# One TensorE loop over all steps, and output stores held back, in a short-sequence attention kernel

## The chip, the core and the metric

One core of a Trainium2 chip runs the kernel. The metric is the time of one execution in microseconds (us), as the device counts it; lower is better. Each figure comes from several executions, beside executions of the kernel before on the same chip. The profile is one execution; its span, from first to last instruction, is 2.0 to 2.7 us shorter than the time of the same execution. Executions differ by about 1% here (153.42 to 155.17 us for the kernel before). One that is over 1.5% above the fastest of its kernel is called slow and set aside in ratios. The records call the profiled execution of the kernel before slow by this rule, yet its 153.69 us lies within its timed range of 153.42 to 155.17.

## The reference

```python
batch, n_heads, seq, head_dim = 32, 12, 128, 64        # float32 q, k, v
scores = scale * np.matmul(q, k.transpose(0, 1, 3, 2))
attn = np.exp(scores - max(scores)); attn /= attn.sum(-1)
return np.matmul(attn, v)                              # float32
```

There are 384 independent heads: 37.75 MB to read, 12.58 MB to write.

## The kernel before

The work is cut into 48 units of 8 heads and 12 groups of 4 units. GpSimd (POOL) issues the loads of q, k and v, which land as bf16; SyncE (SP) issues the stores. In each step TensorE does four things for different units: transposes of q or k (T), an ordering of v by a selection matrix (V), scores (S) and products (O). ScalarE (ACT) does the exponentials and copies v out of PSUM, the memory that TensorE writes its results to. VectorE (DVE) pairs q or k for the transpose, copies transposes out, and divides by the sum.

TensorE's program has three parts: unrolled first steps, a loop of 5 trips of 8 steps, and an unrolled special end of 8 steps, in which two of the last four v are ordered in the transposes' bank, VectorE copies all four out, and the products of the last two units go to the score banks. Its instructions name fixed buffers, so each buffer count must fit a trip of 8 steps.

```python
vgroups = [4] * (NU // 4 - 1) + [2, 2]          # two small v groups at the end, in slots of their own
PERIOD, LOOP0, TRIPS = 8, 0, 5
...
v_at.setdefault({0: -2, 1: -1, 2: -1}.get(m, m - 3), []).append(m)
NQ, NVB, NVE, NP, NT, NA, NO = 8, 2, 8, 4, 2, 8, 6        # NVB: v buffers, NO: output buffers
...
# SP: a store waits only for the division of its units
op("SP", ("store", c), emit, [("N", first + w) for w in range(n)])
# POOL: loads in one order; a v load waits until TensorE has used the group two earlier
loads.append((t_step[s, j, 0] - 2, "qk"[j], s))
loads.append((vstep_of[m] - 1.5 if m in vstep_of else NU + m, "v", g))
...
def tensor_program():                            # cut
    for i in range(a): run("PE", ops[i], plan[i])
    with nc.tensor.Fori(0, TRIPS):
        for i in range(a, a + size): run("PE", ops[i], plan[i])
    for i in range(b, len(ops)): run("PE", ops[i], plan[i])
```

The softmax here doesn't subtract the row's maximum and nothing guards it: scores larger than these inputs give would overflow.

## Time and profile before

| | before |
|---|---|
| time, median (range) | 154.28 us (153.42 to 155.17) |
| span of the profile | 151.1 us |
| v of units 40 to 43 is there (VectorE's wait for it ends) | 120.3 us |
| TensorE starts step 40 | 127.8 us |
| last multiply on VectorE ends | 146.6 us |
| instruction blocks on queue q8 | 8 |

Two more cuts of this profile matter later. The first is TensorE's timeline in the unrolled end: start, duration, engine, line, operation, output<-inputs, count, and in brackets the idle time before and what ended it (PEq is TensorE's own instruction queue; "issue" means that it waited for nothing that the profile shows). The second is VectorE's last wait for v, and its last instruction.

```profile
127.76 0.61 PE L172 MATMUL qk_ps<-ident,pair 128*128 128x128 bf16 x8
...
132.67 0.61 PE L172 MATMUL qk_ps<-ident,pair 128*128 128x128 bf16 x8 [0.82 <-PEq L551]
...
134.15 1.01 PE L172 MATMUL qk_ps<-ident,pair 128*128 128x128 bf16 x8 [0.51 <-PEq L551]
```

```profile
120.28 0.43 DVE L250 COPY pair<-k_b 128x1024 bf16<-128x1024 bf16 x1 [1.32 <-DMA v_b<-in_v_dram]
...
145.93 0.69 DVE L271 TENSOR_TENSOR o_sb<-s_ps,recip 128x512 f32<-128x512 f32 x1
```

The last three transposes are 4.9 and 1.5 us apart, where the loop takes one each 1.8 us. From step 40 (127.76) to the last multiply's end (146.62) are 18.9 us. I use these two marks for every run: **step 40** says roughly how far the loads let the kernel get, the rest is the **end**. The second mark is a convention: the last load that sets the pace before step 40 is v of units 40 to 43, which arrived 7.5 us earlier.

### The profile page before, as it was taken

What the parts mean: (1) busy time and instruction counts of PE and PEld (TensorE: products, weight loads), DVE (VectorE), ACT (ScalarE), POOL (GpSimd) and SP (SyncE); (2) the same over time, 40 slices, a digit from 0 to 9 for tenths busy, and PEclk for the clock granted to TensorE, in tenths of its full rate; (3) what the DMA queues carried; (4) which work ended last, traced back from release to release, by engine and by line L of the source; (5) the groups of instructions that cost most, each with busy time, mean ns of one, the idle gap of its engine ahead of it and who ended that gap; (6) DMA issues with size and microseconds to landing.
All of it is one profiled execution on the core that took longest, in us unless ns stands there. A gap on an engine that the chain in (4) does not pass through costs nothing. (4 is left out here: it accounts for less than half of the span.)

```text
span 151.1 us, 6998 instructions
## 1 busy us (share of the span) xinstructions
PE 103.6 (69%) x3136; PEld 74.0 (49%) x3136; DVE 92.9 (62%) x208; ACT 72.2 (48%) x93; POOL 27.1 (18%) x42
## 2 busy tenths in 40 slices
PE   0057698836829979919949949949469979557810
PEld 0044465624616756606736736637346657347700
DVE  2163335927726969457667677589096599844770
ACT  3000266618433785734744834838605858714600
POOL 6900014005003232050050050050540000000000
PEclk9999999999996999996995987999955999965995
DMA  2999999996999999999999999999999999971344
GB/s 10 204 202 212 207 211 136 196 234 102 237 228 233 208 203 227 243 239 236 246 236 239 244 237 238 244 235 240 242 235 242 241 239 241 331 240 33 113 138 144
DMA packets 25947, 31.62 MB, mean 209 GB/s; under 512 B 1360, under 2 KB 19792, under 8 KB 25936
## 3 DMA queue, kind: packets, MB, share of 16 engines
q0 software_dynamic: 12880, 18.88, 71.0%
q1 hardware_dynamic: 13056, 12.59, 28.6%
q8 instruction: 8, 0.13, 0.3%
q14 instruction: 3, 0.02, 0.0%
HBM read 37.75 MB, written 12.58 MB: 333 GB/s over the span
## 5 line engine op out<-in xcount | busy, mean ns | idle before, releaser
L233 ACT CAST v_e<-v_ps 128x512 bf16<-128x512 f32 x44 | 25.8, 587 | 63.0 <-PE v_ps L186 63.0
L238 ACT ACTIVATE attnT<-s_ps 128x1024 bf16<-128x1024 f32 x48 | 49.3, 1028 | 6.9 <-PE s_ps L212 6.8
L172 PE MATMUL qk_ps<-ident,pair 128*128 128x128 bf16 x384 | 35.3, 246 | 13.3 <-PEq L551 13.0
L224 PE MATMUL o_ps<-v_e,attnT 128*32 128x65 bf16 x1472 | 22.6, 204 | 26.4 <-PEq L551 18.0
L259 DVE COPY qkT<-qk_ps 128x1024 bf16<-128x1024 bf16 x48 | 32.8, 684 | 6.1 <-PE qk_ps L172 6.0
L172 PEld LDWEIGHTS qk_ps<-ident,pair 128*128 128x128 bf16 x384 | 26.5, 110 | 17.7 <-issue 15.7
L186 PE MATMUL v_ps<-v_b,sel 128*32 128x256 bf16 (+1 forms) x768 | 33.6, 306 | 0.8 <-PEq L551 0.8
L271 DVE TENSOR_TENSOR o_sb<-o_ps,recip 128x512 f32<-128x512 f32 x46 | 31.8, 691 | 1.6
L224 PEld LDWEIGHTS o_ps<-v_e,attnT 128*32 128x32 bf16 x1472 | 16.2, 102 | 32.9 <-issue 29.8
L423 POOL DMA_DIRECT2D v_b<-in_v_dram x13 | 9.7, 752 | 82.7 <-PE v_ps L186 82.7
L250 DVE COPY pair<-k_b 128x1024 bf16<-128x1024 bf16 x24 | 10.8, 454 | 19.4 <-DMA v_b<-in_v_dram 19.1
L186 PEld LDWEIGHTS v_ps<-v_b,sel 128*32 128x32 bf16 x768 | 17.5, 106 | 8.2 <-issue 3.4
L212 PE MATMUL s_ps<-qkT 64*128 64x128 bf16 x384 | 20.9, 236 | 0.0
L268 DVE RECIPROCAL recip<-o_ps 128x8 f32<-128x8 f32 x46 | 9.4, 204 | 17.4 <-PE o_ps L224 17.2
L212 PEld LDWEIGHTS s_ps<-qkT 64*128 64x128 bf16 x384 | 12.1, 101 | 11.0 <-issue 10.7
L250 DVE COPY pair<-q_b 128x1024 bf16<-128x1024 bf16 x24 | 10.3, 431 | 4.6 <-DMA q_b<-in_q_dram 4.5
L438 POOL DMA_DIRECT2D q_b<-in_q_dram x12 | 8.7, 725 | 1.0 <-SPq L93 1.0
L438 POOL DMA_DIRECT2D k_b<-in_k_dram x12 | 8.8, 732 | 0.0
L233 DVE CAST v_e<-v_ps 128x512 bf16<-128x512 f32 x2 | 1.4, 694 | 1.1 <-PE v_ps L186 1.0
L233 DVE CAST v_e<-qk_ps 128x512 bf16<-128x512 f32 x2 | 1.4, 693 | 0.6 <-PE qk_ps L186 0.6
L233 ACT ACT_TABLE_LOAD x1 | 1.3, 1283 | 0.9 <-SPq L93 0.9
L186 PE MATMUL qk_ps<-v_b,sel 128*32 128x128 bf16 x64 | 1.7, 266 | 0.0
(14 smaller groups left out, 6.5 us busy)
## 6 DMA issues: line engine op xcount, KB each, us to landing
out_dram<-o_sb SPq DMA_DIRECT2D x48, 256.0 KB, 8.3
q_b<-in_q_dram POOLq DMA_DIRECT2D x12, 512.0 KB, 13.3
k_b<-in_k_dram POOLq DMA_DIRECT2D x12, 512.0 KB, 16.0
v_b<-in_v_dram POOLq DMA_DIRECT2D x11, 512.0 KB, 11.0
v_b<-in_v_dram POOLq DMA_DIRECT2D x2, 256.0 KB, 19.9
```

The lines of the kernel that those rows point to most:

```text
L172: i = nc.tensor.transpose(p[:, :, r4, jj, :], x[:, r].rearrange("p a d -> p (a d)"), ident[:])
L186: x = nc.tensor.matmul(t[r4 * 32:(r4 + 1) * 32, i, :, :], lhsT=pick[:, w * nh + i, jv, :], rhs=v_b[v_slot(g)][:, :n, (4 * jv + r4) * D:(4 ...
L212: i = nc.tensor.matmul(t[:, a, h, :], lhsT=x[p, 1, 4 * w + h, :], rhs=x[p, 0, 4 * w + h, :], start=True, stop=True)
L224: y = nc.tensor.matmul(t[h * SO:(h + 1) * SO, a, r * (D + 1):(r + 1) * (D + 1)], lhsT=x[:, a, h, r * SO:(r + 1) * SO], rhs=v_e[m % NVE][:, ...
L233: return put(v_e[m % NVE][:, :, :D], v_bank(m).rearrange("p (n e) -> p n e", e=D))
L238: return nc.scalar.activation(out=attnT[u % NA][:].rearrange("p a h (r s j) -> p (a h r) s j", r=4, j=J), in_=s_ps[u % 2][:].rearrange("p ...
L250: return nc.vector.tensor_copy(pair[t_index[t] % NP][:], src[:, 8 * b:8 * b + 8])
L259: return nc.vector.tensor_copy(x.rearrange("p h (r j s) -> p (h r) j s", r=4, j=J)[:, :, 2 * b:2 * b + 2, :].rearrange("p x j s -> p x (j ...
L268: nc.vector.reciprocal(r[:], o4[:, :, :, D]).then_inc(s_r, 1)
L271: return nc.vector.tensor_mul(o[:, :, w, :].rearrange("p a (r d) -> p a r d", d=D), o4[:, :, :, :D], r[:].unsqueeze(3).to_broadcast([128, ...
L423: op("POOL", ("load", kind, x), lambda: nc.gpsimd.dma_start(out=v_b[v_slot(x)][:, :n, :], in_=src,).then_inc(s_v[v_slot(x)], 16), deps)
L438: nc.gpsimd.dma_start(out=t, in_=rows[R][:, n:n + 2, :]).then_inc(sm[x % NQ], 16)
```

## The change

It does two things. TensorE runs all steps in one loop of 7 trips, which branches over the parts that a trip lacks, so fewer instructions should have to be fetched (8 instruction blocks on q8 so far) and the special end goes. Stores go out 14 units late, at unit 36 at the latest, so that loads have the DMA to themselves at first. The core of the diff (cut):

```diff
-    vgroups = [4] * (NU // 4 - 1) + [2, 2]
+    vgroups = [4] * (NU // 4)
-    PERIOD, LOOP0, TRIPS = 8, 0, 5
+    PERIOD = 8
+    TRIPS = NU // PERIOD + 1
...
-        if m < NU - 4:
-            v_at.setdefault({0: -2, 1: -1, 2: -1}.get(m, m - 3), []).append(m)
+        v_at[m - 3] = [m]
-    NQ, NVB, NVE, NP, NT, NA, NO = 8, 2, 8, 4, 2, 8, 6
+    NQ, NVB, NVE, NP, NT, NA, NO = 8, 2, 8, 4, 2, 4, 10
+    LATE, LOADED = 14, NU - 12
...
-        op("SP", ("store", c), emit, [("N", first + w) for w in range(n)])
+        last = first + n - 1
+        op("SP", ("store", c), emit, [("N", max(last, min(last + LATE, LOADED)))])
...
-    (special end of 8 steps: 45 lines)
...
+        nc.tensor.reg_mov(trip, 0)
         with nc.tensor.Fori(0, TRIPS):
-            for i in range(a, a + size):
-                run("PE", ops[i], plan[i])
-        for i in range(b, len(ops)):
-            run("PE", ops[i], plan[i])
+            for skipped, always, some in places:
+                run_waits("PE", always)
+                with nc.tensor.If_ne(trip, skipped):
+                    for o, w in some:
+                        run("PE", o, w)
+            nc.tensor.reg_add(trip, trip, 1)
```

More of the change, by code (lines that the diff above doesn't have):

```diff
@@ L62 @@
     of_unit = {u: s for s, (R, f) in enumerate(supers) for u in range(f, f + R // 4)}
-    PERIOD, LOOP0, TRIPS = 8, 0, 5
-    LOOP1 = LOOP0 + PERIOD * TRIPS
-    TAIL = NU - 8
+    PERIOD = 8
+    TRIPS = NU // PERIOD + 1
     t_at, v_at = {}, {}
@@ L78 @@
     for m in range(NU):
-        if m < NU - 4:
-            v_at.setdefault({0: -2, 1: -1, 2: -1}.get(m, m - 3), []).append(m)
-    for u in v_at:
-        v_at[u].sort()
+        v_at[m - 3] = [m]
     steps = range(min(t_at) - 2, NU + 1)
-    NQ, NVB, NVE, NP, NT, NA, NO = 8, 2, 8, 4, 2, 8, 6
+    NQ, NVB, NVE, NP, NT, NA, NO = 8, 2, 8, 4, 2, 4, 10
+    LATE, LOADED = 14, NU - 12
     def sb(name, shape, dtype):
@@ L97 @@
     k_b = [sb(f"k_b{i}", [128, 2, 16 * D], bf16) for i in range(NQ)]
-    v_b = [sb(f"v_b{i}", [128, 4, RV * D], bf16) for i in range(NVB + 2)]
+    v_b = [sb(f"v_b{i}", [128, 4, RV * D], bf16) for i in range(NVB)]
     v_e = [sb(f"v_e{i}", [128, 8, D + 1], bf16) for i in range(NVE)]
@@ L181, in order_v @@
         nh = 8 // n
-        t = v_bank(m).rearrange("p (i n e) -> p i n e", i=nh, e=D)
+        t = v_ps[:].rearrange("p (i n e) -> p i n e", i=nh, e=D)
         for i in range(nh):
@@ L188, in order_v @@
                         lhsT=pick[:, w * nh + i, jv, :],
-                        rhs=v_b[v_slot(g)][:, :n, (4 * jv + r4) * D:(4 * jv + r4 + 1) * D],
+                        rhs=v_b[g % NVB][:, :n, (4 * jv + r4) * D:(4 * jv + r4 + 1) * D],
                         start=jv == 0, stop=jv == 1)
@@ L206, in scores @@
         w = u - supers[s][1]
-        x = qkT[t_slot(s)]
+        x = qkT[s % NT]
         t = s_ps[u % 2][:].rearrange("p a (h x) -> p a h x", h=4)
@@ L218, in values @@
         x = attnT[u % NA]
-        t = o_bank(u)
+        t = o_ps
         for a in range(2):
@@ L228, in values, with keep_v @@
         return y
-    def keep_v(engine, m):
-        put = nc.scalar.copy if engine == "ACT" else nc.vector.tensor_copy
-        return put(v_e[m % NVE][:, :, :D], v_bank(m).rearrange("p (n e) -> p n e", e=D))
+    def keep_v(m):
+        return nc.scalar.copy(v_e[m % NVE][:, :, :D], v_ps[:].rearrange("p (n e) -> p n e", e=D))
     def exps(u):
@@ L246, in pair_up @@
         src = (q_b, k_b)[j][s % NQ][:].rearrange("p a (r d) -> p r a d", d=D)
-        if supers[s][0] == 8:
-            src = (q_b, k_b)[j][s % NQ][:].rearrange("p a e -> p (a e)")[:, :2 * 8 * D].rearrange(
-                "p (a r d) -> p r a d", a=2, d=D)
         return nc.vector.tensor_copy(pair[t_index[t] % NP][:], src[:, 8 * b:8 * b + 8])
@@ L255, in keep_qk @@
         J = R // 4
-        x = qkT[t_slot(s)][:, j, :R, :]
+        x = qkT[s % NT][:, j, :R, :]
         if J == 2:
@@ L265, in normalise @@
         c, w, n, first = splace[u]
-        o4 = o_bank(u)[:, :, :RO * (D + 1)].rearrange("p a (r e) -> p a r e", e=D + 1)
+        o4 = o_ps[:, :, :RO * (D + 1)].rearrange("p a (r e) -> p a r e", e=D + 1)
         r = recip[u % 2]
@@ L274, in normalise @@
             r[:].unsqueeze(3).to_broadcast([128, 2, RO, D]))
-    def v_bank(m):
-        return qk_ps[:].bitcast(f32) if m in (NU - 3, NU - 1) else v_ps[:]
-    def o_bank(u):
-        return s_ps[u % 2] if u >= NU - 2 else o_ps
-    def t_slot(s):
-        return s % NT
-    def v_slot(g):
-        return g % NVB if vgroups[g] == 4 else NVB + g - (len(vgroups) - 2)
     t_order = [t for u in steps for t in t_at.get(u, [])]
@@ L292 @@
     t_step = {t: u for u in steps for t in t_at.get(u, [])}
-    v_order = [m for u in steps for m in v_at.get(u, [])] + list(range(NU - 4, NU))
-    v_before = {m: v_order[i - 1] if i else None for i, m in enumerate(v_order)}
-    v_engine = {m: "ACT" for m in range(NU)}
-    v_engine.update({m: "DVE" for m in range(NU - 4, NU)})
-    v_looped = {vplace[m][0]: u for u in v_at for m in v_at[u] if vplace[m][1] == 0 and LOOP0 <= u < LOOP1}
     vstep_of = {m: u for u in v_at for m in v_at[u]}
@@ L300 @@
     s_k = [tc.alloc_semaphore(f"s_k{i}") for i in range(NQ)]
-    s_v = [tc.alloc_semaphore(f"s_v{i}") for i in range(len(v_b))]
+    s_v = [tc.alloc_semaphore(f"s_v{i}") for i in range(NVB)]
     s_o = [tc.alloc_semaphore(f"s_o{i}") for i in range(NO)]
-    v_landed, landed, v_readers, slot_users = {}, {}, {}, {}
-    for g in range(len(vgroups)):
-        slot_users.setdefault(v_slot(g), []).append(g)
-        v_landed[g] = (s_v[v_slot(g)], 16 * len(slot_users[v_slot(g)]))
+    v_readers = {}
     for u in range(NU):
@@ L315, in pe_transposes, with pe_wait @@
         op("PE", ("T", t), lambda: transposes(t), deps, ["pe_dve"])
+    def pe_wait(kind, key):
+        op("PE", (kind, None), None, [key])
     def pe_order_v(m):
         g, w, n, first = vplace[m]
-        deps, dma = [], []
-        if m == NU - 3:
-            deps.append(("E", t_order[-1]))
-        elif m >= NU - 2:
-            deps.append(("K", m - 2))
-        elif v_before[m] is not None:
-            deps.append(("K", v_before[m]))
-        if w == 0:
-            if g in v_looped:
-                deps.append(("P", t_at[vstep_of[m]][0]))
-            else:
-                dma.append(v_landed[g])
-        op("PE", ("V", m), lambda: order_v(m), deps,
-           ["pe_act" if v_engine[m] == "ACT" else "pe_dve"], dma)
+        deps = [("K", m - 1)] + ([("P", t_at[vstep_of[m]][0])] if w == 0 else [])
+        op("PE", ("V", m), lambda: order_v(m), deps, ["pe_act"])
     def pe_scores(u):
@@ L343, in pe_values, with act_keep @@
         deps += [("K", m) for m in sorted({v_at_head(u, a, h)[0] for a in range(2) for h in range(4)})]
-        if u < NU - 2:
-            deps.append(("N", u - 1))
+        deps.append(("N", u - 1))
         op("PE", ("O", u), lambda: values(u), deps, ["pe_dve"])
-    def keep(m):
-        e = v_engine[m]
+    def act_keep(m):
         deps = [("V", m)]
@@ L352, in keep @@
             deps += [("O", u) for u in v_readers[m - NVE]]
-        op(e, ("K", m), lambda: keep_v(e, m), deps, ["act_pe" if e == "ACT" else "dve_pe"])
+        op("ACT", ("K", m), lambda: keep_v(m), deps, ["act_pe"])
     def act_exps(u):
@@ L362, in dve_pair @@
         dma = [((s_q, s_k)[j][s % NQ], 16 * (s // NQ + 1))]
-        for g, u in v_looped.items():
-            if t_at[u][0] == t:
-                dma.append(v_landed[g])
+        for m in v_at.get(t_step[t], []):
+            g, w, n, first = vplace[m]
+            if w == 0:
+                dma.append((s_v[g % NVB], 16 * (g // NVB + 1)))
         op("DVE", ("P", t), lambda: pair_up(t), deps, ["dve_io"] if t_index[t] else ["dve_pe", "dve_io"], dma)
@@ L371, in dve_keep @@
         for x in range(s):
-            if t_slot(x) == t_slot(s):
+            if x % NT == s % NT:
                 R, f = supers[x]
@@ L381, in dve_normalise @@
             dma.append((s_o[c % NO], sum(16 * pieces(x) for x in range(c % NO, c, NO))))
-        marks = ["dve_pe"] if u < NU - 3 else []
-        if u + 1 > TAIL:
-            marks = marks + ["dve_io"]
+        marks = ["dve_pe"] + (["dve_io"] if u + 8 > t_step[t_order[-1]] else [])
         op("DVE", ("N", u), lambda: normalise(u), [("O", u)], marks, dma)
@@ L412, in pool_load @@
         if kind == "v":
-            users = slot_users[v_slot(x)]
-            i = users.index(x)
-            if i:
-                g = users[i - 1]
-                first = sum(vgroups[:g])
-                deps = [("V", first + w) for w in range(vgroups[g])]
+            if x >= NVB:
+                deps = [("V", sum(vgroups[:x - NVB + 1]) - 1)]
             n, first = vgroups[x], sum(vgroups[:x])
-            src = v_rows[:, first:first + n, :]
-            if n == 2:
-                src = v_rows[:, NU - 4:, :].rearrange("p (a w) e -> p w a e", a=2)[:, (first - NU + 4) // 2]
             op("POOL", ("load", kind, x), lambda: nc.gpsimd.dma_start(
-                out=v_b[v_slot(x)][:, :n, :], in_=src,
-            ).then_inc(s_v[v_slot(x)], 16), deps)
+                out=v_b[x % NVB][:, :n, :], in_=v_rows[:, first:first + n, :],
+            ).then_inc(s_v[x % NVB], 16), deps)
             return
@@ L434, in emit @@
         def emit():
-            t = bufs[x % NQ][:]
-            if R == 8:
-                t = t.rearrange("p a e -> p (a e)")[:, :2 * R * D].rearrange("p (a e) -> p a e", a=2)
-            nc.gpsimd.dma_start(out=t, in_=rows[R][:, n:n + 2, :]).then_inc(sm[x % NQ], 16)
+            nc.gpsimd.dma_start(
+                out=bufs[x % NQ][:], in_=rows[R][:, n:n + 2, :]).then_inc(sm[x % NQ], 16)
         op("POOL", ("load", kind, x), emit, deps)
-    step_starts = {}
+    op("ACT", ("K", -1), lambda: nc.scalar.drain(), [], ["act_pe"])
+    at_step = {}
     for u in steps:
-        step_starts[u] = len(program["PE"])
-        if u >= TAIL:
-            continue
+        start = len(program["PE"])
         for t in t_at.get(u, []):
             pe_transposes(t)
+        if u == t_step[t_order[-1]] + 1:
+            pe_wait("T", ("E", t_order[-1]))
         for m in v_at.get(u, []):
             pe_order_v(m)
-            keep(m)
-        if u == -1:
-            pe_scores(0)
-            act_exps(0)
-        if 0 <= u:
+            act_keep(m)
+        if u - 1 == vstep_of[NU - 1]:
+            pe_wait("V", ("K", NU - 1))
+        if 0 <= u + 1 < NU:
             pe_scores(u + 1)
             act_exps(u + 1)
+        if 0 <= u < NU:
             pe_values(u)
@@ L465 @@
             dve_keep(t)
-        if u + 2 <= TAIL:
-            for t in t_at.get(u + 2, []):
-                dve_pair(t)
-    def tail_scores(u):
-        pe_scores(u)
-        act_exps(u)
-    t45, t46, t47 = t_order[-3:]
-    u = TAIL
-    dve_normalise(u - 1)
-    pe_transposes(t45)
-    dve_keep(t45)
-    pe_order_v(u + 3)
-    tail_scores(u + 1)
-    pe_values(u)
-    dve_normalise(u)
-    keep(u + 3)
-    dve_pair(t46)
-    tail_scores(u + 2)
-    pe_values(u + 1)
-    dve_pair(t47)
-    tail_scores(u + 3)
-    dve_normalise(u + 1)
-    pe_transposes(t46)
-    dve_keep(t46)
-    pe_values(u + 2)
-    pe_transposes(t47)
-    dve_keep(t47)
-    dve_normalise(u + 2)
-    pe_values(u + 3)
-    tail_scores(u + 4)
-    tail_scores(u + 5)
-    dve_normalise(u + 3)
-    pe_order_v(u + 4)
-    keep(u + 4)
-    pe_order_v(u + 5)
-    keep(u + 5)
-    tail_scores(u + 6)
-    pe_values(u + 4)
-    dve_normalise(u + 4)
-    pe_order_v(u + 6)
-    keep(u + 6)
-    tail_scores(u + 7)
-    pe_values(u + 5)
-    pe_order_v(u + 7)
-    keep(u + 7)
-    dve_normalise(u + 5)
-    pe_values(u + 6)
-    dve_normalise(u + 6)
-    pe_values(u + 7)
-    dve_normalise(u + 7)
+        for t in t_at.get(u + 2, []):
+            dve_pair(t)
+        for o in program["PE"][start:]:
+            at_step[o.key] = u
     for c in range(len(stores)):
@@ L528 @@
         m = sum(vgroups[:g])
-        loads.append((vstep_of[m] - 1.5 if m in vstep_of else NU + m, "v", g))
+        loads.append((vstep_of[m] - 1.5, "v", g))
     loads.sort(key=lambda e: e[0])
@@ L546, in waits_of, with run_waits @@
         return out
+    def run_waits(engine, waits):
+        for name, value in waits:
+            i = ENGINE[engine].wait_ge(sems[name], value)
+            if engine == "PE":
+                i.then_inc(sems[name], -value)
     def run(engine, o, waits):
         e = ENGINE[engine]
-        for name, value in waits:
-            i = e.wait_ge(sems[name], value)
-            if engine == "PE":
-                i.then_inc(sems[name], -value)
+        run_waits(engine, waits)
         for s, value in o.dma:
@@ L560, in tensor_program @@
     def tensor_program():
-        ops = program["PE"]
-        a, b = step_starts[LOOP0], step_starts[LOOP1]
-        assert (b - a) % TRIPS == 0
-        size = (b - a) // TRIPS
-        plan = [waits_of("PE", o) for o in ops]
-        for i in range(a, b):
-            assert not ops[i].dma and plan[i] == plan[a + (i - a) % size], (ops[i].key, plan[i])
-            assert ops[i].key[0] == ops[a + (i - a) % size].key[0]
-        for i in range(a):
-            run("PE", ops[i], plan[i])
-        with nc.tensor.Fori(0, TRIPS):
-            for i in range(a, a + size):
-                run("PE", ops[i], plan[i])
-        for i in range(b, len(ops)):
-            run("PE", ops[i], plan[i])
+        ops, waits, when = {}, {}, {}
+        for o in program["PE"]:
+            place = at_step[o.key] % PERIOD, o.key[0]
+            w = waits_of("PE", o)
+            assert waits.setdefault(place, w) == w and not o.dma, (o.key, w, waits[place])
+            when.setdefault(place, []).append((at_step[o.key] // PERIOD + 1, o.emit is None))
+            if at_step[o.key] // PERIOD == 2:
+                ops[place] = o
+        places = []
+        for place in [(l, kind) for l in range(PERIOD) for kind in "TVSO"]:
+            trips = [t for t, empty in when[place] if not empty]
+            assert trips in (list(range(TRIPS - 1)), list(range(1, TRIPS))), (place, trips)
+            waiting = len(when[place]) > len(trips)
+            assert not waiting or len(when[place]) == TRIPS
+            skipped = 0 if trips[0] else TRIPS - 1
+            if waiting or not places or places[-1][0] != skipped:
+                places.append((skipped, waits[place] if waiting else [], []))
+            places[-1][2].append((ops[place], [] if waiting else waits[place]))
+        trip = ctx.enter_context(nc.tensor.register("trip"))
+        nc.tensor.reg_mov(trip, 0)
+        with nc.tensor.Fori(0, TRIPS):
+            for skipped, always, some in places:
[4 more added lines that the diff above has]
+            nc.tensor.reg_add(trip, trip, 1)
     with nc.Block() as block:
```

## The prediction

> **What bounds the kernel now.** I read the 40 slices first, then 5 us windows over the whole span, then the waits, then TensorE's timeline. The page's slices of data movement and the queues:
>
> ```profile
> DMA  2999999996999999999999999999999999971344
> GB/s 10 204 202 212 207 211 136 196 234 102 237 228 233 208 203 227 243 239 236 246 236 239 244 237 238 244 235 240 242 235 242 241 239 241 331 240 33 113 138 144
> q0 software_dynamic: 12880, 18.88, 71.0%
> q1 hardware_dynamic: 13056, 12.59, 28.6%
> q8 instruction: 8, 0.13, 0.3%
> ```
>
> A slice is 3.78 us. The DMA engines are full from slice 1 to slice 34 (about 132 us), with a hole at slice 9, then mostly idle for the last 19 us. q0 is the loads (18.88 MB as they land in bf16), q1 the stores (12.59 MB). The windows (columns: stretch, length, busy us and count of PE, PEld, DVE, ACT, POOL, granted clock, DMA share, GB/s) give the rates:
>
> ```profile
> 5.00:10.00 5.00, 1.78 (x16) 1.55 (x16) 2.12 (x4) 0.00 (x0) 2.66 (x4) 1.00 1.14 204
> 10.00:15.00 5.00, 3.24 (x35) 2.00 (x32) 2.35 (x5) 0.00 (x0) 0.00 (x0) 1.00 1.16 211
> 15.00:20.00 5.00, 3.68 (x50) 2.29 (x51) 1.84 (x4) 1.77 (x4) 0.00 (x0) 1.00 1.18 208
> ...
> 95.00:100.00 5.00, 3.04 (x99) 2.10 (x99) 2.75 (x7) 3.67 (x5) 2.00 (x3) 1.00 1.14 241
> ...
> 130.00:135.00 5.00, 2.58 (x88) 2.11 (x88) 2.96 (x6) 2.74 (x4) 0.00 (x0) 0.86 1.00 338
> 135.00:140.00 5.00, 3.29 (x114) 2.87 (x112) 2.89 (x6) 1.91 (x2) 0.00 (x0) 0.50 0.14 43
> 140.00:145.00 5.00, 3.65 (x220) 2.76 (x212) 4.04 (x9) 2.08 (x3) 0.00 (x0) 0.95 0.23 76
> 145.00:150.00 5.00, 0.00 (x0) 0.00 (x0) 1.55 (x4) 0.00 (x0) 0.00 (x0) 0.73 0.62 210
> ```
>
> The first store is issued at 25.0 us, so the first three rows are loads alone: mean 208 GB/s. 130 to 135 us is stores alone: 338 GB/s. Mixed 1.5 to 1 these rates give 1/(0.6/208 + 0.4/338) = 246 GB/s, and 235 to 246 is what the middle shows: **load time and store time simply add up.** Loads cost 18.88/0.208 = 90.8 us, stores 12.59/0.338 = 37.2 us, 0.78 us for each of the 48 units. The first 5 us moved 54 x 5 = 0.27 MB, as if loading began at 3.7 us. A DMA that never idled would end at 3.7 + 90.8 + 37.2 = 131.7 us. The span is 151.1 us, so 19.4 us are DMA idleness, over half of it after 135 us, where TensorE and VectorE finish the last units and there is nothing to move.
>
> In the middle, compute waits for loads (the waits):
>
> ```profile
> POOL v_b L423 <- PE v_ps L186: 82.7, 9, 14.5
> DVE pair L250 <- DMA v_b<-in_v_dram: 19.1, 9, 3.7
> ```
>
> Each group of 4 units waits once, about 2 us, for its v load; POOL can issue that load only when TensorE has used the group two earlier. TensorE's timeline shows its pace and its instruction stalls:
>
> ```profile
> 29.42 0.34 PE L224 MATMUL o_ps<-v_e,attnT 128*32 128x65 bf16 x19
> 32.84 0.30 PE L224 MATMUL o_ps<-v_e,attnT 128*32 128x65 bf16 x13 [3.08 <-issue]
> ...
> 62.08 0.43 PE L224 MATMUL o_ps<-v_e,attnT 128*32 128x65 bf16 x32
> 62.67 0.61 PE L172 MATMUL qk_ps<-ident,pair 128*128 128x128 bf16 x8 [0.16 <-PEq L551]
> ...
> 125.89 0.61 PE L172 MATMUL qk_ps<-ident,pair 128*128 128x128 bf16 x8
> ```
>
> In the first trip the 32 products of one step stop in the middle, with nothing in the program to wait for: 0.65, 3.08, 1.68 and 3.02 us, in steps 1, 3, 5 and 7, after 23, 19, 15 and 11 products. Later trips never do it. Free of waits a step takes 1.80 us.
>
> [...] A load packet is 1466 bytes (18.88 MB/12880), 7.0 us per 1000 packets at 208 GB/s, a store packet 964 bytes, 2.9 us, so where both queues are full I estimate that loads get some 70% of the time. [...] q8 is 8 packets of 16 KB; the stalls lie two steps apart, and two steps are some 264 instructions; the loop of some 1056 stalls only in its first trip. From entering one block (the end of the former stall) to the arrival of the next I read 6.8, 5.4 and 6.8 us under load. [...] The back edge in the trace: from the start of one step's products to the next step's transposes is normally 0.36 us, but 0.59 us at 62.08 and 0.58 at 85.42 and 105.59, so about 0.2 us is exposed once a trip.
>
> **The change part by part.**
>
> 1. *One loop of 7 trips.* Merging neighbours with the same condition leaves 12 branches a trip (one for steps 0 to 2 of the trip, two each in steps 3 and 4, three in step 5, two each in steps 6 and 7). [...] In the middle this is hidden: 4 steps take 7.2 us of compute against some 10.9 us of DMA. It shows in the first 14 steps, where loads alone allow 90.8/12 = 7.6 us per 4 steps: I charge 2 us. It also shows in the last steps: 1 us. Instruction blocks fall from 8 to 5 or 6, and the 8.4 us of mid-group stalls go: that fetching moves into trip 0, partly under the wait for the first load.
>
> 2. *The start.* v unit 0 now goes through the copy of step -3, which must wait for the v load. Before, its products started at 13.95 us, when that load was in; the transpose of that step began at 11.13. Chaining 1.0 us pieces from there[...] I get scores of unit 0 at 20.3 us instead of 19.3, and the last block of the loop, fetched from about 16 us on, comes at about 22: another 2 us. The fourth v is then ordered at about 25 us instead of 21.8, and with it the ninth load is issued. The first 8 loads last till 3.7 + 8 x 2.52 = 24 us. So the DMA is dry for about 3 us, where before it lost 1 to 2 us here and 2 us more at 35 to 40 us (141 GB/s instead of 241). Call it even, with 4 us idle in the start and point 1 together.
>
> 3. *Stores held back.* A chunk goes out 14 units late, but at unit 36 at the latest. Till unit 36 stores of 22 units are out (17.1 us of DMA); 14 units go out in one burst there, 12 follow. The bytes are the same; they leave the stretch in which loads gate compute and fill the one in which the DMA was idle. The 10 output buffers cover it: a buffer is needed again 5 steps (13 us) after its store was issued, and the median store lands in 8.3 us.
>
> 4. *The end.* The last v load (units 44 to 47) now waits for v of unit 39, because two equal slots replace the two small extra ones, so it competes with the burst. When it lands, loads (90.8 us), 22 units of stores (17.1) and some 3 units of the burst (2.4) have passed: 3.7 + 110.3 + 5 us idle (4 from point 2, 1 in between) = **119 us**. From there VectorE has three full steps at 1.80 us and six at about 1.65 (products 0.5 until the reciprocal, 0.93 for it and the multiply, some 0.2 for the wait back), 15.3 us, plus 1 us of branches. Then the last store: 4.5 us, as from 146.6 to 151.1 now. Sum 119 + 15.3 + 1 + 4.5 = 139.8. The DMA's own end: 23 units left at 0.78 us = 17.9 us, 137. The two ends nearly meet, and the special ending that used both score banks for products (steps of 1 us) isn't missed much. I take a span of **139 us**, 12 less than now. Time minus span was 153.69 - 151.1 = 2.6 us in the profiled run, 3.8 for the median; 3 more gives **142 us**.
>
> **The rivals.**
>
> *Stores were hidden anyway.* If the loads had gaps, holding stores back would free nothing: the end would move only by the restructured tail, 150 to 157 us. Against it: DMA share at 1.1 and more, and rates that add up.
>
> *Instruction fetch becomes the bound in trip 0.* The taken branches may each stall for a block, not only the last; three or four stalls at 5.4 to 6.8 us instead of one short one would delay the start by up to 10 us: 148 to 152 us. [...] Against: the first load lands only at 6.8 us and early DMA traffic is light.
>
> *The end becomes a new wait.* If the burst starves the last v load, or VectorE waits for an output buffer that is still being stored, the last steps slip by 3 to 5 us: 145 to 147. For it: stores of 3.67 MB (10.9 us) stand in the queue at that moment. Against: the estimated 70% share, and the load is half way at least.
>
> *The loads-only phase is compute-bound.* Branches at 0.3 us or more would idle the DMA another 3 us: 145.
>
> **Range and chances.** Everything well (no dry DMA at the start, branches hidden) gives 3.7 + 128 + about 2 for the last receipt = 134 of span, 137 of time. One of the last three rivals gives 145 to 148. So 8 in 10: 136.5 to 148. Faster by over 2% (under 151.8) needs a quarter of the expected gain: 0.93; within 2%: 0.05; slower: 0.02.
>
> **What would show it.** q8 with 5 or 6 packets; no mid-group stop after step 0; 208 GB/s till the first store at about 50 to 55 us, then about 240, then 300 and more from about 112 us almost to the end, DMA slices full till the last two; VectorE's last wait for v at about 119 us; the last unit's multiply at about 135. It is wrong if the DMA is dry for more than 5 us early (fetch, late ninth load), if the last v lands after 124 us, or if a wait for stores shows up on VectorE.

## The result

The changed kernel takes 144.36 us (143.38 to 145.38, 4 runs) against 154.28 us. The ratio is 0.9357, with a 95% interval of 0.9258 to 0.9456: faster. A ratio here is the mean time of one kernel's fast runs over that of the other's of the same rounds, so not quite the ratio of the medians quoted.

The slices (now 3.53 us each) and queues of the changed kernel:

```profile
DMA  2999999699999999999999999999999999999982
GB/s 14 186 206 211 202 206 179 81 210 188 181 200 143 212 189 187 219 176 235 246 236 240 253 236 240 252 235 242 253 235 241 255 206 313 379 382 369 335 281 77
q0 software_dynamic: 12864, 18.88, 76.5%
q1 hardware_dynamic: 13056, 12.59, 28.0%
q8 instruction: 4, 0.07, 0.2%
```

The DMA now works until two slices before the end. The first store is issued at 57.1 us. In the windows the last stretch moves stores alone, faster than I had read before:

```profile
20.00:25.00 5.00, 4.43 (x92) 2.89 (x92) 1.60 (x4) 2.42 (x4) 0.59 (x1) 0.66 0.95 179
25.00:30.00 5.00, 4.80 (x161) 3.37 (x158) 4.90 (x11) 3.89 (x6) 1.56 (x3) 1.00 0.85 130
...
40.00:45.00 5.00, 3.74 (x141) 2.79 (x145) 4.90 (x12) 2.87 (x5) 2.02 (x3) 1.00 0.97 165
...
120.00:125.00 5.00, 3.42 (x108) 2.47 (x112) 3.41 (x8) 2.20 (x4) 0.00 (x0) 1.00 1.09 380
```

But the loads-only stretch has dips (130 and 165 GB/s), though nothing but loads is there to move. The waits (total, times, longest) show why loads are not ordered faster, and one new wait, for output buffers:

```profile
POOL v_b L381 <- PE v_ps L185: 83.4, 10, 16.7
...
DVE pair L245 <- DMA v_b<-in_v_dram: 20.2, 12, 2.9
...
DVE recip L263 <- DMA out_dram<-o_sb: 6.3, 6, 2.1
```

TensorE's timeline has one stop in the middle of a group, in the step before step 0, in place of four; step 40 begins at 120.07 us:

```profile
20.57 1.04 PE L185 MATMUL v_ps<-v_b,sel 128*32 128x256 bf16 x15 [2.15 <-issue]
...
120.07 0.61 PE L171 MATMUL qk_ps<-ident,pair 128*128 128x128 bf16 x8 [0.46 <-PEq L458]
```

VectorE's timeline shows the arrival of v of units 40 to 43, that of the last v load and the last multiply:

```profile
110.36 0.43 DVE L245 COPY pair<-k_b 128x1024 bf16<-128x1024 bf16 x1 [1.67 <-DMA v_b<-in_v_dram]
...
121.25 0.43 DVE L245 COPY pair<-k_b 128x1024 bf16<-128x1024 bf16 x1 [1.33 <-DMA v_b<-in_v_dram]
...
136.17 0.69 DVE L266 TENSOR_TENSOR o_sb<-o_ps,recip 128x512 f32<-128x512 f32 x1
```

So of the 9.8 us of span, 7.7 are gained on the way to step 40 (127.76 to 120.07) and 2.1 in the end (18.9 to 16.8 us). The split depends on the mark: v of units 40 to 43 is there 9.9 us earlier (120.28 and 110.36), and from there to the last multiply's end both kernels take much the same, 26.3 and 26.5 us. By that mark the whole gain lies ahead of it, and the end gains nothing. The last store takes 4.4 us (4.5 before). Which part of the change bought them is what the experiments ask.

### The profile page after: what moved, and what is told of

It is laid out like the page before. It is cut to its first block, busy times and chain, and to the rows that moved or that the text cites. A ratio compares the mean times of both kernels' runs of the same rounds, so it can differ in the third digit from the quotient of the medians.

```text
span 141.3 us, 6998 instructions
## 1 busy us (share of the span) xinstructions
PE 97.5 (69%) x3072; PEld 68.9 (49%) x3072; DVE 89.8 (64%) x204; ACT 74.2 (52%) x97; POOL 26.8 (19%) x41
## 3 DMA queue, kind: packets, MB, share of 16 engines
q0 software_dynamic: 12864, 18.88, 76.5%
## 5 line engine op out<-in xcount | busy, mean ns | idle before, releaser
L231 ACT CAST v_e<-v_ps 128x512 bf16<-128x512 f32 x48 | 28.2, 588 | 58.4 <-PE v_ps L185 58.4
L171 PE MATMUL qk_ps<-ident,pair 128*128 128x128 bf16 x384 | 32.5, 233 | 16.5 <-PEq L458 15.7
L185 PE MATMUL v_ps<-v_b,sel 128*32 128x256 bf16 x768 | 33.0, 295 | 3.1 <-issue 2.1
L171 PEld LDWEIGHTS qk_ps<-ident,pair 128*128 128x128 bf16 x384 | 24.3, 104 | 21.5 <-issue 20.6
L266 DVE TENSOR_TENSOR o_sb<-o_ps,recip 128x512 f32<-128x512 f32 x48 | 33.2, 691 | 1.7
L223 PE MATMUL o_ps<-v_e,attnT 128*32 128x65 bf16 x1536 | 21.7, 200 | 18.2 <-PEq L458 18.1
L381 POOL DMA_DIRECT2D v_b<-in_v_dram x12 | 9.2, 770 | 83.4 <-PE v_ps L185 83.4
L245 DVE COPY pair<-k_b 128x1024 bf16<-128x1024 bf16 x24 | 11.0, 460 | 20.2 <-DMA v_b<-in_v_dram 20.2
L211 PE MATMUL s_ps<-qkT 64*128 64x128 bf16 x384 | 19.9, 226 | 0.6 <-PEq L458 0.5
L211 PEld LDWEIGHTS s_ps<-qkT 64*128 64x128 bf16 x384 | 11.3, 97 | 11.5 <-issue 11.5
```

The source lines that it names most:

```text
L171: i = nc.tensor.transpose(p[:, :, r4, jj, :], x[:, r].rearrange("p a d -> p (a d)"), ident[:])
L185: x = nc.tensor.matmul(t[r4 * 32:(r4 + 1) * 32, i, :, :], lhsT=pick[:, w * nh + i, jv, :], rhs=v_b[g % NVB][:, :n, (4 * jv + r4) * D:(4 * ...
L211: i = nc.tensor.matmul(t[:, a, h, :], lhsT=x[p, 1, 4 * w + h, :], rhs=x[p, 0, 4 * w + h, :], start=True, stop=True)
L223: y = nc.tensor.matmul(t[h * SO:(h + 1) * SO, a, r * (D + 1):(r + 1) * (D + 1)], lhsT=x[:, a, h, r * SO:(r + 1) * SO], rhs=v_e[m % NVE][:, ...
L231: return nc.scalar.copy(v_e[m % NVE][:, :, :D], v_ps[:].rearrange("p (n e) -> p n e", e=D))
L245: return nc.vector.tensor_copy(pair[t_index[t] % NP][:], src[:, 8 * b:8 * b + 8])
```

## The experiments

All gave correct results. They ran in four sets (e1 to e3 and e5; e4, its control, e6 and e7; e8 to e10; e11), on three chips; each set has its own runs of the kernel before, so compare ratios. "Step 40" is the start of its transposes, "end" the time from there to the last multiply's end, both from the one profiled run.

| run | median us | before us | ratio (95%) | step 40 | end |
|---|---|---|---|---|---|
| kernel before | 154.28 | | 1 | 127.8 | 18.9 |
| changed | 144.36 | 154.28 | 0.936 (0.926 to 0.946) | 120.1 | 16.8 |
| e1 loop, not held | 151.08 | 153.19 | 0.981 (0.972 to 0.990) | 128.6 | 16.9 |
| e2 held, no loop | 152.28 | 153.19 | 0.995 (0.984 to 1.006) | 125.4 | 20.2 |
| e3 held 7 | 147.31 | 153.19 | 0.962 (0.954 to 0.969) | 123.3 | 17.8 |
| e5 14 buffers | 143.19 | 153.19 | 0.927 (0.916 to 0.937) | 119.7 * | 17.9 * |
| e6 first steps out | 146.73 | 154.39 | 0.949 (0.932 to 0.966) | 121.9 | 16.9 |
| e10 the same, not held | 151.92 | 154.20 | 0.991 (0.983 to 0.999) | 129.3 * | 18.0 * |
| e7 held 20 | 143.60 | 154.39 | 0.932 (0.922 to 0.943) | 116.0 | 16.4 |
| e8 q, k earlier | 144.03 | 154.20 | 0.941 (0.935 to 0.946) | 120.0 | 15.5 |
| e9 both e6 and e8 | 148.44 | 154.20 | 0.971 (0.963 to 0.979) | 124.4 | 15.5 |

(* profiled run called slow.) Three more runs are told below. The granted clock of TensorE differs between the runs too: 0.90 to 0.95 in the four of the changed kernel, 0.85 to 0.90 in those of e1. Within e1 the run with the higher clock is the faster (149.86 us at 0.900, 152.53 at 0.849), within the changed kernel it is not (143.77 at 0.902, 145.38 at 0.923). What the clock adds to small differences was not separated.

### e1: the loop alone

```diff
-    LATE, LOADED = 14, NU - 12
+    LATE, LOADED = 0, NU - 12
```

> The changed kernel with stores issued at once (no unit of delay), TensorE still in one loop. Theory A (the stores that are held back pay: their DMA time moves from the load-bound stretch into an idle end; the loop is about neutral): the last v load lands 39 units of stores into the run instead of 25, 3.7 + 90.8 + 30.4 + 5 idle = 130 us, then 15.6 us of steps and 4.4 us of last store: span 150, time 150 to 156. Theory B (the single loop pays: no stops for instructions in the first trip, a smoother end): time stays at 144 to 147.

Measured: 151.08 us, span 149.7; the last v load at 129.8 us. Theory A expected just that. Without the holding, the loop (with the v groups and buffer counts that come with it) is worth 1.9%. Where, its one profile doesn't settle: its span is 1.4 us shorter. From step 40 the end is 2.0 us shorter (16.9 against 18.9) and step 40 comes 0.8 later; but v of units 40 to 43 is there 1.3 us earlier (118.98 against 120.28), and from there both take much the same, 26.5 and 26.3 us.

### e2: the holding alone

The kernel before with the `LATE` lines, 10 output buffers, and VectorE's signals to SP placed as in the changed kernel (cut):

```diff
+    LATE, LOADED = 14, NU - 12                     # and NO = 10
-        op("SP", ("store", c), emit, [("N", first + w) for w in range(n)])
+        last = first + n - 1
+        op("SP", ("store", c), emit, [("N", max(last, min(last + LATE, LOADED)))])
```

> The kernel before with only the stores held back 14 units (till unit 36) and 10 output buffers; TensorE keeps its unrolled first and last steps and its four stops for instructions. Theory A: most of the gain is here, 141 to 147 us, the loads end about 118 us. Theory B: 152 to 155.

Measured: 152.28 us, ratio 0.995, not clear of 1. Theory A was wrong here: holding alone gains almost nothing. Yet e1 had refuted theory B. **The parts do not add: 0.5% and 1.9% alone, 6.4% together.** In its profile e2 is 4.7 us ahead of the kernel before when v of units 40 to 43 is there, and gives 3.6 of them back after that: 29.9 us to the last multiply's end, against 26.3.

```profile
115.60 0.43 DVE L252 COPY pair<-k_b 128x1024 bf16<-128x1024 bf16 x1 [1.67 <-DMA v_b<-in_v_dram]
```

The slices of e2 (3.76 us each):

```profile
GB/s 7 203 198 214 205 213 157 195 151 19 182 209 20 146 210 166 188 185 240 236 248 244 237 238 243 237 240 242 237 242 240 237 244 349 382 381 381 170 161 118
```

Slices 9 and 12 move almost nothing, and TensorE's timeline has stops just ahead of them:

```profile
26.10 0.26 PE L226 MATMUL o_ps<-v_e,attnT 128*32 128x65 bf16 x9 [0.92 <-issue]
...
33.20 0.30 PE L226 MATMUL o_ps<-v_e,attnT 128*32 128x65 bf16 x13 [3.33 <-issue]
...
44.58 0.51 PE L226 MATMUL o_ps<-v_e,attnT 128*32 128x65 bf16 x21 [2.62 <-issue]
```

Between 20 and 50 us e2 moves 136 GB/s, the changed kernel 176: over 30 us that is 1.2 MB, or 5.8 us of loading at the 208 GB/s of the first stretch. Both have only loads to move there. The kernel before moves 200 GB/s in the same stretch and e1 202, because stores fill up what loads leave. By queue it is plainer (`--dma --window 20:50`): the kernel before loads 3.96 MB there and e2 4.01, with no store in the way; e1 loads 4.33 and the changed kernel 5.27. So e2 takes the stores out of this stretch and puts holes in their place. That the stops are fetches of instructions the trace shows: in the kernel before, the packets of the instruction queue (q8) start at 23.67, 30.41, 35.87 and 42.67 us, and TensorE goes on 2.3 to 2.4 us after each, at 26.00, 32.84, 38.28 and 45.05. My theory for the next runs (C) was that these stops make the holes.

### e3: half the delay

```diff
-    LATE, LOADED = 14, NU - 12
+    LATE, LOADED = 7, NU - 12
```

> The changed kernel with a delay of 7 units instead of 14. Theory A: linear, 8 more units of stores (30 instead of 22) lie ahead of the last v load, 8 x 0.78 = 6 us: 148.5 to 151, last v at about 127. If the gain has a threshold (loads only need some of the relief), 144 to 146.

Measured: 147.31 us; the last v load at 124.8 us. Not held, held 7 and held 14 have the ratios 0.981, 0.962 and 0.936: 1.9 and 2.6 points for 7 units each, with intervals of 1 point on each. (The medians, 151.08, 147.31 and 144.36, come from two sets and give 3.8 and 2.9 us, the other way round.) Within the one-loop kernel the holding pays about evenly; no threshold shows. The time is 1.2 us under theory A's range, and the last v load came 2.2 us earlier than it said.

### e5: enough output buffers

```diff
-    NQ, NVB, NVE, NP, NT, NA, NO = 8, 2, 8, 4, 2, 4, 10
+    NQ, NVB, NVE, NP, NT, NA, NO = 8, 2, 8, 4, 2, 4, 14
```

> The changed kernel with 14 output buffers instead of 10, so that VectorE no longer waits for stores (6.3 us in 6 waits in the trace). Theory A: these waits lie ahead of a wait for v that would come anyway, so the time stays 143 to 145.5. Rival: they hold TensorE back and with it the next v load: 139 to 142.

Measured: 143.19 us (141.23 to 144.69). The waits for stores are gone from the list, but its interval overlaps that of the changed kernel, and it has runs on both sides of theory and rival. A gain of 1% from more buffers is neither shown nor excluded; a gain anywhere near the 6.3 us of waiting is excluded.

### e6 and e10: the first steps out of the loop

The first steps stand unrolled ahead of a loop of 6 trips with 6 branches each, so that the loop's blocks are fetched in steps 0 to 7 again, as before the change. The end stays in the loop. e10 is e6 with `LATE = 0`.

```diff
-        with nc.tensor.Fori(0, TRIPS):
+        for o, w in prefix:
+            run("PE", o, w)
+        nc.tensor.reg_mov(trip, 1)
+        with nc.tensor.Fori(0, TRIPS - 1):
             for skipped, always, some in places:
                 run_waits("PE", always)
+                if skipped == 0:
+                    for o, w in some:
+                        run("PE", o, w)
+                    continue
```

> The changed kernel, but TensorE's steps before step 0 stand unrolled ahead of the loop (6 trips, 6 branches a trip), as before the change; stores stay held back, the last steps stay in the loop. So the loop's instruction blocks are again fetched during steps 0 to 7. Theory C (held stores leave the DMA nothing to do while TensorE stops for instructions, which is why holding alone gained only 0.5%): three or four stops of 1 to 3.5 us in the middle of a group come back, the transposes of step 40 start about 5 us later than the 120.1 us of the changed kernel, time 147.5 to 150. Rival D (the unrolled end is what spoiled the kernel that only held back; the stops at the start don't matter): 143.5 to 145.5.

> Steps before the loop unrolled (stops for instructions in steps 0 to 7), stores not held back, last steps in the loop. With the three others of this kind it makes a square: stops or none, held or not. Theory C (stops hurt only where no stores fill the DMA): it is within 1 us of the single loop without holding (151.1): 150 to 152. If stops cost the same with and without holding: 153 to 154.5.

Measured: 146.73 us for e6, 151.92 for e10. The stops came back in e6, and the holes with them (slices of 3.6 us; slices 9 and 12 again):

```profile
GB/s 7 194 206 211 207 205 203 207 175 63 209 171 28 206 206 133 198 228 235 236 234 245 235 240 243 238 244 245 235 240 244 237 238 289 381 379 380 381 291 26
```

```profile
24.16 0.27 PE L223 MATMUL o_ps<-v_e,attnT 128*32 128x65 bf16 x10 [1.05 <-issue]
30.69 0.30 PE L223 MATMUL o_ps<-v_e,attnT 128*32 128x65 bf16 x15 [2.60 <-issue]
...
41.49 0.39 PE L223 MATMUL o_ps<-v_e,attnT 128*32 128x65 bf16 x25 [2.05 <-issue]
```

But they delay step 40 by 1.8 us, not by the 5 that theory C needed (by ratio the two kernels' intervals overlap), and e6 keeps most of the gain of holding (146.73 against 151.92). The reason is that the loop pays for its instructions too, only earlier. The ninth load, which waits for TensorE, is ordered at 20.8 us in e6 and at 24.4 in the changed kernel, after the single stop; eight steps later (two v loads on) it is 43.95 against 39.80. So e6 loses 7.8 us in steps 0 to 7 but starts 3.6 us earlier. The four runs make a square:

| | stops in steps 0 to 7 | one stop, before step 0 | difference |
|---|---|---|---|
| not held | 151.92 (e10) | 151.08 (e1) | 0.8 us |
| held 14 | 146.73 (e6) | 144.36 (changed) | 2.4 us |

By ratios the differences are 1.0 and 1.3 points, with intervals of 1 point and more on each, so this square does not show that stops hurt more when stores are held. **Theory C, as the whole cause of e2, falls.** The stops make the holes, but they are the smaller part of what e2 lacks. By queue, holding lets 0.70 MB more of loads through between 20 and 50 us with the stops (e10 4.02, e6 4.72) and 0.94 without (e1 4.33, changed 5.27), where in the unrolled kernel it let through 0.05 more.

What separates e2 from e6 (152.28 and 146.73 us, both held, both with stops)? The profiles give two parts. The end: 20.2 us against 16.9 (the special end with held stores against the plain one; the special end without them took 18.9). And step 40: 125.4 against 121.9. That second difference is there at once: the ninth load is ordered at 22.3 us against 20.8, and two v loads later it is 47.5 against 44.0; from there to the order of v of units 40 to 43 both take 57 us. e2 differs from e6 ahead of that point, as far as I see, in the placement of the first v orderings (steps -2, -1, -1 against -3, -2, -1), in the length of its stops (6.9 us against 5.7 in all) and in the buffers of the exponentials. How much belongs to each was not separated.

### e7: held longer

```diff
-    NQ, NVB, NVE, NP, NT, NA, NO = 8, 2, 8, 4, 2, 4, 10
-    LATE, LOADED = 14, NU - 12
+    NQ, NVB, NVE, NP, NT, NA, NO = 8, 2, 8, 4, 2, 4, 14
+    LATE, LOADED = 20, NU - 12
```

> Stores held back 20 units, with 14 buffers. If load time and store time simply add up, 6 units fewer lie ahead of the last v load: it lands 4 to 5 us earlier (116 to 118). But 32 units of stores then have to drain behind it: 32 x 0.69 us at 380 GB/s are 22 us, so the end is set by stores, 141 to 144 (hardly a gain). If the loads-only stretch is bound by TensorE and VectorE instead of the DMA, the last v load comes less than 2 us earlier and the time is 143 to 145.

Measured: 143.60 us, ratio 0.932, no different from 14 units. In its profile the last v load and the last multiply come 4 to 5 us earlier than in the changed kernel, but the span is 141.6 us, 0.3 more:

```profile
116.93 0.43 DVE L245 COPY pair<-k_b 128x1024 bf16<-128x1024 bf16 x1 [1.12 <-DMA v_b<-in_v_dram]
...
131.67 0.69 DVE L266 TENSOR_TENSOR o_sb<-o_ps,recip 128x512 f32<-128x512 f32 x1
```

From the last multiply to the end are now 9.2 us, which the DMA spends on the heap of stores. The buffers alone (e5, held 14) had shown no clear gain. Fourteen is about where the end of compute and the end of the stores meet; beyond it the gain turns into a wait for stores.

### e4 and its control: three v buffers

The dips of the changed kernel in the loads-only stretch come, I thought, from v loads that wait for one of two buffers. With three, the loop body must be 12 steps long:

```diff
-    PERIOD = 8
+    PERIOD = 12
-    NQ, NVB, NVE, NP, NT, NA, NO = 8, 2, 8, 4, 2, 4, 10
+    NQ, NVB, NVE, NP, NT, NA, NO = 8, 3, 12, 4, 3, 4, 10
```

> The changed kernel with three v buffers (and, so that one loop body fits, trips of 12 steps, three transposed buffers, 12 v outputs). Theory E (the DMA dips to 130 GB/s at 25 to 30 us and 165 at 40 to 45 because a v load is ordered only when the group two earlier has been used): the dips go, the last v lands earlier, 138 to 141.5. Rival: TensorE's larger body (1600 instructions, 7 blocks) costs in trip 0 what that brings: 144 to 147.

> Control of the one above: the same three buffers and 12-step trips, but each v load still waits for the group two earlier. Its distance to the changed kernel is the price of the larger body (0 to +3 us: 144 to 147.5), its distance to the one above is the worth of ordering v one group earlier (theory E: 4 to 6 us; rival: under 1).

Measured: 153.43 us, and 153.74 for the control, whose v loads wait for the group two earlier as in the changed kernel. Both miss every expectation. The queue and TensorE's timeline of e4:

```profile
q8 instruction: 12, 0.20, 0.5%
```

```profile
36.52 0.40 PE L185 MATMUL v_ps<-v_b,sel 128*32 128x256 bf16 x2 [2.90 <-issue]
...
48.41 0.51 PE L185 MATMUL v_ps<-v_b,sel 128*32 128x256 bf16 x11 [1.98 <-issue]
...
61.08 0.82 PE L171 MATMUL qk_ps<-ident,pair 128*128 128x128 bf16 x6 [4.48 <-issue]
```

Twelve blocks instead of 4, and stops on till 61 us. The longer body costs some 9 us (153.74 against 144.36); under that, the third buffer shows nothing. What it would be worth without the longer body stays open.

### e8, e9 and e11: a fuller queue of loads

The same idea without another buffer: q and k loads (8 buffers each) are ordered one group earlier, so that they do not stand behind the v load that waits.

```diff
-            loads.append((t_step[s, j, 0] - 2, "qk"[j], s))
+            loads.append((t_step[s, j, 0] - (2 if s < 3 else 6), "qk"[j], s))
```

> The changed kernel with one line different: from the fourth on, q and k loads are ordered one group (4 steps) earlier, so that they no longer stand behind the v load that waits for a slot; the first loads keep their order. Theory E (the DMA runs dry at 20 to 30 and 40 to 45 us because loads queue up behind that wait): 10 loads instead of 8 carry it to 29 us, the dips to 81 and 143 GB/s go, the transposes of step 40 start at 116 to 118 instead of 120.1 us, time 140 to 142.5. Rival: a v load now lands later because more stands ahead of it, and TensorE waits for it as long as it gained: 143.5 to 146.

> The same line, on the kernel with the steps before the loop unrolled (146.7 us). If the stops for instructions cost time only by drying up the queue of loads, a fuller queue takes most of their cost away: 141 to 143.5, as good as the one above or better, for its start is 3.6 us earlier. If they cost time by delaying TensorE itself, 145 to 147.

Measured: 144.03 us for e8, which is the rival's number. The slices of e8 (3.54 us each) and VectorE's last wait for v:

```profile
GB/s 13 194 198 206 208 206 211 211 207 211 205 212 128 191 208 163 191 176 232 234 243 246 236 237 245 238 238 244 239 237 248 237 151 237 380 380 380 379 307 8
```

```profile
120.10 0.43 DVE L245 COPY pair<-k_b 128x1024 bf16<-128x1024 bf16 x1 [0.29 <-DMA v_b<-in_v_dram]
```

The early dips are gone: 205 GB/s and more from slice 3 through 11, and 198 GB/s from 20 to 50 us against 176, which is 0.66 MB or 3.2 us of loading ahead. But step 40 starts where it did (120.0 us). The lead lay in q and k buffers. v, which decides, stood behind them: the fifth v load is ordered at 43.6 us instead of 39.8. And when q and k had run out, the last v load was alone in the queue and the DMA partly idle (125 GB/s from 112 to 118 us).

e9, with the first steps out of the loop as well, took 148.44 us, no better than e6 with 146.73 (by ratio 0.971 against 0.949, intervals that just overlap). So a fuller queue does not take away the price of the stops. That they delay TensorE itself, and cost more with q and k ahead of v, fits but was not shown. That was neither of the two numbers expected.

The last run let the stores of e8 go at unit 34 to fill the late hole:

```diff
-    LATE, LOADED = 14, NU - 12
+    LATE, LOADED = 14, NU - 14
```

> q and k ordered one group earlier, and the held stores let go at unit 34 instead of 36. In the kernel that only ordered q and k earlier the early dip was gone, but from 112 to 118 us the DMA moved 35 to 223 GB/s: the last v load stood alone there and the burst came 2 to 3 us too late. Theory E (each us of an idle DMA before the last store costs a us): the burst at about 109.6 us fills the hole, DMA and compute end 1.5 to 2 us sooner, 141 to 143 us. Rival: the burst now slows the v load before the last and moves everything behind it: 144 to 146.

Measured: median 144.1 us (141.44 to 146.02, 7 runs) against 155.24 us. The hole was filled only in part (150 GB/s instead of 125 in that stretch) and step 40 starts at 120.3 us. The ratio of its fast runs is 0.912, but only 3 of 7 runs count as fast; the ratio of the medians is 0.928. Whether it beats the changed kernel by 1% or not at all is not settled.

## Why the prediction was right, and where its steps failed

The time (144.4 us for 142 predicted) lies in the range, and the direction and size are right. By its steps (the last 3 us of the sum, from span to time, were a little too many: the 3.8 us for the median took one execution's span from another's time; each execution's own gap is 2.0 to 2.7 us, 2.1 in the profiled run):

- **The end.** Right. From the last v load to the last multiply's end I added 15.3 us and 1 us for branches; it took 15.6 (121.25 to 136.86). The steps there took 1.6 us each (products at 128.74, 130.34, 131.92, 133.49), and the last store 4.4 for 4.5. (The "about 2 for the last receipt" in the prediction's range is in the trace of the kernel before: its last bytes move at 149.05 us and the span ends at 151.12, 2.1 us later.) "The special ending isn't missed much" holds: from step 40 the special end took 18.9 and 20.2 us in its two profiles, the plain one 15.5 to 18.0 in all nine of the table; but counted from v of units 40 to 43 the kernel before took 26.3 us, e1 and the changed kernel 26.5.
- **When the last v lands.** Predicted 119, measured 121.25. The mis-sized term is the idle DMA, 5 us in the sum. What had moved by then is as counted (18.88 MB of loads, and 6.57 MB of stores, which are the 25 units), so 3.7 + 110.3 = 114.0 leaves 7.2. I expected 208 GB/s until the first store; from 20 to 57 us it was 130 to 203, mean 179, which makes some 5.2 us of the shortfall; part of it is idle time, part a lower rate of a full DMA (188 GB/s at a share of 1.12 from 50 to 57 us). Stores cost less than at the 338 GB/s of the sum; at the 380 measured when they are alone, the shortfall would be 9.4 us. The 2 us charged for TensorE's branches there were an estimate, and fit: from step 1 to step 8 it took 13.61 us for seven steps, 1.94 each against 1.80, 1.0 us for seven steps.
- **The start.** Scores of unit 0 came at 21.5 us (predicted 20.3 with up to 2 us of stop), the ninth load was ordered at 24.4 (25), one stop of 2.15 us before step 0, with 4 instruction blocks fetched (I had said 5 or 6). Right. But the reason was half wrong: the later placement of v's first ordering shows no cost. With the first steps unrolled (e6) the same placement orders the ninth load at 20.8, before the 22.2 of the kernel before. The loop's first trip makes the difference to 24.4, 3.6 us: 2.2 are the stop, and most of the rest is that groups of matmuls after it took 1.03 us where those of e6 took 0.62.
- **Load time and store time add up.** Right inside the one-loop kernel: e1 landed its last v at 129.8 us for 130 expected, e7 at 116.9 for 116 to 118, and the stores then set the end as expected. But only roughly: e1's number still had the 5 us of idle DMA that was 7.2 in the changed kernel, so its fit is in part luck, and e3 landed at 124.8 for 127. Wrong as a claim about the holding by itself: in e2 the stores that left were not followed by loads between 20 and 50 us (4.01 MB for 3.96). That TensorE freed v buffers too slowly there is argued, not shown. The prediction treated the parts as a sum; they do not add.
- **The share of loads beside the burst.** Estimated at 70%, and too high: from 112 to 120.8 us, with the last v load and the burst in the queues, the packets of loads took 57.2% of the 16 engines' span and those of stores 55.6%, about half each. The estimate supposes one load packet (1466 bytes) for each store packet (964), which was not shown: in this window 679 packets of loads stand beside 1645 of stores. The last v load took 10 us all the same (ordered at 110.74, there at 121.25).
- **The rivals.** Stores hidden anyway: false in this kernel; in e2 the time hardly moved, though its loads came up to 4.7 us earlier. Fetch as the bound in trip 0: false with 8 steps to a trip (one stop, 2.15 us), true with 12 (e4: stops of 1.83 to 4.48 us till 61.08 us, and 153.43 us). A new wait for stores on VectorE: it came (6.3 us), but its cost is below what e5 resolves. Of the three signs of being wrong it was the third, and not a good one; the first, a DMA dry for over 5 us early, was about reached (5.2 us short between 20 and 57 us, though never dry for long); the second, v after 124 us, did not come.

Open are what makes the first 8 steps of e2 3.5 us slower than those of e6, why the unrolled end takes 3.6 us longer when stores are held, and the worth of a third v buffer.

## What to carry to other kernels

Moving stores out of a transfer-bound stretch paid here only where what remained could use the time: between 20 and 50 us the changed kernel loaded 5.27 MB against the 4.33 of e1, while e2 loaded 4.01 against the 3.96 of the kernel before. So look first at whether loads are ordered early enough, and at what stops the engine that frees their buffers. Hold back as much as the tail of compute can hide and no more: beyond that, the stores are the tail (held 20 units, 9.2 us from the last multiply to the end, and a ratio of 0.932 for 0.936). Loading ahead what does not decide (q and k here) raised the GB/s, from 176 to 198 between 20 and 50 us, and not the speed (0.941 for 0.936).

## What the traces show of fetches, branches and stores

- Instruction fetch. In the changed kernel an 8-step body (about 1,060 instructions, by my count of 132 a step, and the branches) came in 4 packets of 16 KB on q8, at 2.33, 11.99, 18.11 and 23.99 us, with one stop of 2.15 us; then no packet came on q8 and TensorE had no more stops of this kind. In e4 a 12-step body (about 1,600 and the branches) took 12 packets, and the last stop ended at 61.08 us. The cost was not hidden: in the kernel before the packets came 5.5 to 6.8 us apart between 23.67 and 42.67 us (DMA share 1.02 from 20 to 50 us), and in these three kernels TensorE stood 0.65 to 4.48 us at a stop.
- Branches. In the trace of the changed kernel the 84 of the conditional parts (`--source L496`) take 63 ns in the median and 343 at most, the loop's own mostly 209 ns (before: 207 to 235 in four of five). Twelve parts at 63 and one back edge at 209, as many as lie between step 1 and step 8, make 1.0 us: as much as those seven steps took over 1.80 each.
- Stores to HBM. In DMAs of 256 KB and packets of about 1 KB they ran at 380 GB/s when alone (120 to 125 us of the changed kernel, DMA share 1.09). My 338 from the kernel before was a stretch with a share of 1.00.
